# Two projections of a layer as one 2x2 block product with seven products, and the work around it in another order

## The chip, the cores and the metric

The kernel runs on one core of a Trainium2 chip. The metric is the device time of one execution in microseconds. The kernel before takes 1845.83 us, the median of three runs (1845.75 to 1846.41). TensorE (PE) multiplies, VectorE (DVE) and ScalarE (ACT) work elementwise, GpSimd (POOL) does small work and issues some DMAs, SyncE (SP) issues the other DMAs. Each engine works through its own queue in a fixed order.

## The reference

One sequence of 512 tokens, width 1024, float32, goes through a first block (an mLSTM beside a stick-breaking attention, then an MLP of width 4096) and then through two hybrid layers. The change is in the hybrid layers:

```python
h = rms_norm_2(x, g_pre)
proj = jnp.einsum('bsd,de->bse', h, w_in)
q_h, f_h, i_h, z_h, q_a, k_a, v_a, z_a = jnp.split(proj, SPLIT_POINTS, axis=-1)
o_h = hgrn2(q_h, f_h, i_h, lb)           # 8 recurrent heads of 128
o_h = rms_norm_2(o_h, g_head).reshape(B, S, HG_WIDTH) * jax.nn.silu(z_h)
...                                      # rotary on q_a, k_a
o_a = sliding_window_attention(q_a, k_a, v_a, sinks) * jax.nn.silu(z_a)
y = jnp.einsum('bse,ed->bsd', jnp.concatenate([o_h, o_a], axis=-1), w_out)
return x + rms_norm_2(y, g_post)
```

The parts q, f, i and z of the recurrent heads are 1024 columns each: i holds the values, z the output gate.

## The kernel before, in words

Every float32 operand of a large product is split into two halves of reduced precision, hi and lo, and a product is three matmuls (hi by hi, hi by lo, lo by hi) that add up in one PSUM bank (`mm3`, lines 143 to 151). A projection of 512 columns (`gemm_a` gives columns by tokens, `gemm_b` tokens by columns) has four tiles of 128x512, each of 8 parts of the depth: 4 x 8 x 3 = 96 matmuls of 512 columns. The tiles (`mm`) rotate through two PSUM banks, so the third waits until the first has been evacuated.

Weights come in pieces of 512 KB (`wr`, six buffers) by SyncE. ScalarE casts each to its high half (`wh`, line 137) and VectorE subtracts for the low half (`wl`, five buffers, line 138).

In `seven` a product of a 2x2 block matrix of x by a 2x2 block matrix of weights is done with seven block products of 24 matmuls instead of eight, as Strassen's method does, with sums of blocks of x and of the weights. The weight sums are made by DMA: a piece is loaded by SyncE (`piece`, line 181), and GpSimd issues a DMA that adds a second piece onto it in place (`plus`, line 185). The MLP's `down2` uses it three times.

A layer begins while the step before it ends: for each block of 128 tokens, as soon as its last sum is there, `prep` squares it, GpSimd makes the norm's factor (lines 293 and 115), VectorE scales (283), TensorE transposes (286), ScalarE casts the high half `hh` (258) and VectorE makes the low half `hl` (259). In layer 1 the block's sum first gets the layer's norm (716) and the old x, which is read back from memory (715). Then come i(0) (`proj_i`, values, four heads), which goes by token blocks, q(0) and f(0), and then zh(0), i(1), q(1), f(1) with the first four recurrent heads (`hgrn`) beside them at higher priority; key and value, zh(1), q and gate of the attention with the other four heads; the rest with the attention pairs (`swa_pair`); the output product.

The order in each engine's queue is set when the program is built: a scheduler takes priorities (those of evacuations, weight splits and heads are raised) and its own estimate of times. On the chip each queue then runs in that order, whatever is ready.

## Time and profile before

| | |
|---|---|
| time, median of three runs | 1845.83 us |
| the profiled execution | 1846.15 us, span 1844.2 us |
| TensorE busy | 1809.8 us, 98% |
| VectorE, ScalarE, GpSimd busy | 58%, 46%, 9% |
| layer 0, layer 1 | 861 to 1348 us, 1348 to 1844 us |
| DMA, whole span | 195.80 MB, 106 GB/s |

The spans of the layers are read from the first matmul of i(0) and the last of the output product. Matmul records overlap their successors, so the cost of one is the time between two starts, or a stretch without gaps divided by its count.

### The profile page before, as it was taken

How to read it: one execution, taken by the hardware profiler on the slowest of the kernel's cores; microseconds unless marked ns; L12 is line 12 of the kernel's file. 1: busy time of each engine (PE TensorE's matmuls, PEld its weight loads, DVE VectorE, ACT ScalarE, POOL GpSimd, SP SyncE). 2: the span in 40 equal slices, each digit the busy share in tenths (PEclk: the TensorE clock that was granted, in tenths of full speed). 3: DMA queues.
4: the chain of work that ended last, by engine and by line, in shares of the span. 5: the costliest groups of instructions: out<-in, count | busy, mean ns of one | idle time of the engine just before them, and what ended most of it. 6: DMA issues, size and time to landing. Idle time of an engine off the chain costs nothing.

```text
span 1844.2 us, 29460 instructions
## 1 busy us (share of the span) xinstructions
PE 1809.8 (98%) x11624; PEld 1484.8 (81%) x11624; DVE 1069.2 (58%) x2179; ACT 849.8 (46%) x1696; POOL 161.6 (9%) x215
## 2 busy tenths in 40 slices
PE   7999999999999999999999999999999999999998
PEld 5777788787798888878888888888878888888886
DVE  4364445546555575575474766755365648575733
ACT  4546644343443344443343436655343345375741
POOL 1001111020001110110000001100120000101002
PEclk9999999999999999999999999999999999999999
DMA  7342432221425855474331232322352223322222
GB/s 216 70 103 70 97 92 69 69 92 46 149 91 128 204 146 167 122 187 146 94 116 52 87 131 88 103 86 75 110 164 92 88 75 98 127 87 75 75 69 91
DMA packets 111602, 195.80 MB, mean 106 GB/s; under 512 B 9441, under 2 KB 20065, under 8 KB 111465
## 3 DMA queue, kind: packets, MB, share of 16 engines
q1 hardware_dynamic: 104936, 181.35, 31.9%
q0 software_dynamic: 6528, 12.58, 4.0%
q8 instruction: 91, 1.49, 0.3%
q14 instruction: 47, 0.38, 0.1%
HBM read 179.21 MB, written 14.70 MB: 105 GB/s over the span
## 4 chain that ended last, share of the span: by engine, by line
PE 53%; ACT 1%; DVE 1%; issue 0%; POOL 0%; DMA 0%; DVEq 0%; POOLq 0%; SPq 0%; ACTq 0%
PE mm L151 14%; PE mm L150 14%; PE mm L149 13%; PE xc L634 2%; PE xa L602 1%; PE xc L636 1%; PE xb L624 1%; PE xc L498 1%; PE xa L443 1%; PE xb L470 1%; PE xc L490 1%; PE xc L500 1%; PE xb L626 1%; PE xa L432 0%; PE mt L536 0%
## 5 line engine op out<-in xcount | busy, mean ns | idle before, releaser
L138 DVE TENSOR_TENSOR wl<-wr,wh 128x1024 fp32r<-128x1024 f32 (+1 forms) x248 | 298.3, 1211 | 119.6 <-PE mm L150 72.2
L149 PE MATMUL mm<-wh,hh 128*128 128x512 f32 (+1 forms) x896 | 348.2, 389 | 5.8 <-ACT hh L258 3.0
L150 PE MATMUL mm<-wl,hh 128*128 128x512 f32 (+1 forms) x896 | 348.3, 389 | 0.8 <-DVE wl L138 0.8
L151 PE MATMUL mm<-wh,hl 128*128 128x512 f32 (+1 forms) x896 | 346.9, 390 | 0.0
L137 ACT CAST wh<-wr 128x1024 fp32r<-128x1024 f32 (+1 forms) x248 | 255.0, 1038 | 143.8 <-PE mm L151 72.2
L149 PE MATMUL mm<-hh,wh 128*128 128x512 f32 x640 | 254.8, 398 | 1.3 <-ACT pg L801 1.3
L151 PE MATMUL mm<-hh,wl 128*128 128x512 f32 x640 | 253.5, 396 | 1.8 <-DVE wl L138 1.7
L150 PE MATMUL mm<-hl,wh 128*128 128x512 f32 x640 | 253.1, 395 | 0.0
L149 PEld LDWEIGHTS mm<-wh,hh 128*128 128x128 f32 x896 | 169.1, 189 | 40.1 <-ACT hh L258 3.5
L150 PEld LDWEIGHTS mm<-wl,hh 128*128 128x128 f32 x896 | 168.9, 189 | 33.5 <-DVE wl L138 1.7
L151 PEld LDWEIGHTS mm<-wh,hl 128*128 128x128 f32 x896 | 167.8, 189 | 31.4 <-DVE hl L259 0.5
L151 PEld LDWEIGHTS mm<-hh,wl 128*128 128x128 f32 x640 | 120.8, 189 | 28.8 <-DVE wl L138 3.0
L149 PEld LDWEIGHTS mm<-hh,wh 128*128 128x128 f32 x640 | 120.8, 189 | 27.4 <-ACT pg L801 2.6
L150 PEld LDWEIGHTS mm<-hl,wh 128*128 128x128 f32 x640 | 121.0, 189 | 24.9 <-issue 0.2
L149 PE MATMUL mm<-qd,wh 128*128 128x512 f32 (+1 forms) x288 | 105.5, 366 | 0.0
L150 PE MATMUL mm<-qd,wh 128*128 128x512 f32 (+1 forms) x288 | 105.4, 366 | 0.0
L151 PE MATMUL mm<-qd,wl 128*128 128x512 f32 (+1 forms) x288 | 104.9, 365 | 0.0
L115 POOL TENSOR_TENSOR sm<-sm,nhalf 128x4 f32<-128x4 f32 (+1 forms) x64 | 60.2, 941 | 504.6 <-DVE sm L507 327.9
L149 PE MATMUL mm<-wh,qd 128*128 128x512 f32 x192 | 75.2, 392 | 1.2 <-DVE qd L1198 0.8
L151 PE MATMUL mm<-wh,qd 128*128 128x512 f32 x192 | 74.7, 389 | 0.0
L150 PE MATMUL mm<-wl,qd 128*128 128x512 f32 x192 | 74.7, 389 | 0.0
L610 ACT ACTIVATE pg<-pg,sm 128x256 f32<-128x256 f32 (+1 forms) x128 | 60.9, 478 | 15.5 <-DVE sm L608 15.4
(312 smaller groups left out, 2927.8 us busy)
## 6 DMA issues: line engine op xcount, KB each, us to landing
wr<-in_w_in_dram SPq DMA_DIRECT2D x160, 512.0 KB, 4.7
wr<-in_w_out_dram SPq DMA_DIRECT2D x40, 512.0 KB, 4.0
wr<-in_w_down_dram SPq DMA_DIRECT2D x38, 512.0 KB, 5.4
wr<-in_w_up_dram SPq DMA_DIRECT2D x32, 512.0 KB, 5.1
wr<-in_w_down_dram POOLq DMA_DIRECT2D x24, 512.0 KB, 7.8
zh<-pg SPq DMA_DIRECT2D x16, 256.0 KB, 2.0
pg<-zh SPq DMA_DIRECT2D x16, 256.0 KB, 2.8
za<-pg SPq DMA_DIRECT2D x16, 256.0 KB, 2.0
```

Source lines behind the costliest of these rows:

```text
L115: self.nc.gpsimd.tensor_tensor(y, ms, e, ALU.pow)
L137: nc.scalar.copy(hi, raw)
L138: nc.vector.tensor_tensor(lo, raw, hi.bitcast(F32), ALU.subtract)
L149: nc.tensor.matmul(ps, sh, mh, start=(k == 0), stop=False)
L150: nc.tensor.matmul(ps, sh, ml, start=False, stop=False)
L151: nc.tensor.matmul(ps, sl, mh, start=False, stop=(k == n - 1))
L443: nc.tensor.matmul(pl[32 * j:32 * j + 32, o0 + 32 * c:o0 + 32 * c + 32], k[:, o:o + 32], q[:, o:o + 32])
L470: nc.tensor.matmul(pb[0:64, 64 * c:64 * c + 64], k[:, o:o + 64], q[:, o + 64:o + 128])
L490: nc.tensor.matmul(pS[:, c, :], kt[:, c, :], v[c][:, vc])
L498: nc.tensor.matmul(po[:, c, :], ST[:, c, :], v[c][:, vc], start=True, stop=(c == 0))
L610: nc.scalar.activation(prw, prw, AF.Exp, bias=pn[:, n:n + 1], scale=-1.0, accum_out=den[:, n:n + 1])
L634: nc.tensor.matmul(o, va[0][:, n, vv], pT[n // 2][:, n % 2, 0:P], start=True, stop=(n == 0))
```

## The change

In each layer i(c) and zh(c) become one block product, `pair(c)`: x is cut into 2x2 blocks (256 tokens by 512 of depth), the weights into the 512 columns of i and of zh. `pair` has 7 x 24 = 168 matmuls. It needs sums of blocks of x, which `sides` makes once for both pairs of a layer: four whole sums of hi and lo, four sums and differences, four splits, all 128x1024; the results stay in a pool of their own whose space the recurrent heads use later. q(0) comes first in a layer, in two halves of 256 tokens; then `sides`, f(0), pair(0) and pair(1); then q(1) and f(1) with the first heads. The order of weights in the plan of `seven` changes in one place, also for the MLP.

```diff
@@ seven @@
-                ("00", "1", c, True, (0, 0, ALU.add)), ("10", "2", x, True, (0, 0, ALU.add)),
-                ("Y", "6", c, False, (0, 1, ALU.subtract)), ("V", "7", c, False, (1, 1, ALU.subtract)),
+                ("00", "1", c, True, (0, 0, ALU.add)), ("Y", "6", c, False, (0, 1, ALU.subtract)),
+                ("10", "2", x, True, (0, 0, ALU.add)), ("V", "7", c, False, (1, 1, ALU.subtract)),
...
+    def sides(self, T, pool, tmp):
...
+        a11, a12, a21, a22 = raw
+        whole(a21, part(0, 1))
+        whole(a22, part(1, 1))
+        nc.vector.tensor_tensor(a22, a21, a22, ALU.subtract)
+        keep("5", a22)
+        whole(a11, part(0, 0))
+        whole(a12, part(1, 0))
+        nc.vector.tensor_tensor(a22, a22, a11, ALU.subtract)
+        nc.vector.tensor_tensor(a12, a22, a12, ALU.add)
+        keep("3", a12)
+        keep("6", a22)
+        nc.vector.tensor_tensor(a21, a11, a21, ALU.subtract)
+        keep("7", a21)
+        return ops
...
@@ layer, proj_q @@
-            K.gemm_a(win[:, c * S:(c + 1) * S], evac)
+            K.gemm_a(win[:, c * S:(c + 1) * S], evac, 2 if c == 0 else 1)
...
@@ layer, pair in place of proj_i and proj_zh @@
+        def pair(c, ops):
...
+            def acc(i, t, j, ps, op):
+                tb = 2 * i + t
+                if j:
+                    v = quad[:, tb, :]
+                    if tb in seen:
+                        nc.vector.tensor_tensor(v, v, ps, op)
+                    else:
+                        seen.add(tb)
+                        nc.scalar.copy(v, ps)
+                    return
+                z = ps
+                if tb in zc:
+                    z = zc[tb]
+                    nc.vector.tensor_tensor(z, z, ps, op)
...
+            K.seven(blk, ops.get, acc)
...
@@ layer, order @@
-        proj_i(0)
         proj_q(0)
-        proj_f(0)
+        with tc.tile_pool(name="sd", bufs=1, reuse_waits="tile") as sd:
+            ops = K.sides(K.T, sd, [K.quad(), K.quad()])
+            proj_f(0)
+            pair(0, ops)
+            pair(1, ops)
+        K.lp2 = lctx.enter_context(tc.tile_pool(name="lp2", bufs=1, reuse_waits="tile"))
...
         p0 = mark()
-        proj_zh(0)
-        proj_i(1)
         proj_q(1)
         proj_f(1)
...
         proj_kv()
-        proj_zh(1)
         proj_qa(0)
         proj_za(0)
```

How the queues move is shown at three places. VectorE at the start of layer 0, before; the three rows with `mm` as a source are evacuations of q(0)'s tiles, those of line 138 weight splits:

```order
709 L138 TENSOR_TENSOR wl_6878<-wr_6875,wh_6877 128x1024
710 L138 TENSOR_TENSOR wl_6884<-wr_6881,wh_6883 128x1024
711 L138 TENSOR_TENSOR wl_6890<-wr_6887,wh_6889 128x1024
712 L138 TENSOR_TENSOR wl_7009<-wr_7006,wh_7008 128x1024
713 L378 SCALAR_TENSOR_TENSOR qd_6868<-mm_6893,om_6720,pg_6918 128x512
714 L378 SCALAR_TENSOR_TENSOR qd_6868<-mm_6921,om_6720,pg_6946 128x512
715 L378 SCALAR_TENSOR_TENSOR qd_6868<-mm_6949,om_6720,pg_6974 128x512
716 L138 TENSOR_TENSOR wl_7015<-wr_7012,wh_7014 128x1024
717 L138 TENSOR_TENSOR wl_7021<-wr_7018,wh_7020 128x1024
```

VectorE at the same place after the change; line 292 is the low half (259 before), 412 the evacuation of a half tile of q(0) (378 before), 258 a whole sum of x, 346 and 347 the casts of a mask:

```order
688 L292 TENSOR_TENSOR hl_6305<-xb_6639,hh_6303 128x4x128
689 L292 TENSOR_TENSOR hl_6306<-xa_6647,hh_6304 128x4x128
692 L292 TENSOR_TENSOR hl_6305<-xb_6680,hh_6303 128x4x128
693 L292 TENSOR_TENSOR hl_6306<-xa_6688,hh_6304 128x4x128
694 L412 SCALAR_TENSOR_TENSOR qd_6731<-mm_6756,om_6720,pg_6781 128x256
695 L258 TENSOR_TENSOR qd_6984<-hh_6303,hl_6305 128x4x256
696 L258 TENSOR_TENSOR qd_6983<-hh_6303,hl_6305 128x4x256
697 L258 TENSOR_TENSOR qd_6983<-hh_6304,hl_6306 128x4x256
698 L258 TENSOR_TENSOR qd_6984<-hh_6304,hl_6306 128x4x256
699 L346 CAST hgmask<-ST_6701 128x512
700 L347 CAST hgmask<-ST_6703 128x128
701 L412 SCALAR_TENSOR_TENSOR qd_6731<-mm_6784,om_6720,pg_6809 128x256
```

The evacuations of q(0)'s first two tiles now stand behind the low half of block 3, with the four whole sums between them.

VectorE at the start of layer 1, before: the last block's norm and addition of x (716), its scaling (283) and the last low halves (259):

```order
1376 L716 SCALAR_TENSOR_TENSOR pg_10974<-pg_10974,sm_11668,pg_11670 128x512
1377 L716 SCALAR_TENSOR_TENSOR pg_10975<-pg_10975,sm_11668,pg_11674 128x512
1378 L283 SCALAR_TENSOR_TENSOR pg_11678<-pg_10974,sm_11686,pg_11260 128x512
1379 L283 SCALAR_TENSOR_TENSOR pg_11679<-pg_10975,sm_11686,pg_11262 128x512
1380 L259 TENSOR_TENSOR hl_11258<-xb_11621,hh_11256 128x4x128
1381 L259 TENSOR_TENSOR hl_11259<-xa_11629,hh_11257 128x4x128
1382 L259 TENSOR_TENSOR hl_11258<-xb_11689,hh_11256 128x4x128
1383 L259 TENSOR_TENSOR hl_11259<-xa_11697,hh_11257 128x4x128
```

The same place after the change (768 is the norm and the addition of x, 716 before; 316 the scaling):

```order
1420 L768 SCALAR_TENSOR_TENSOR pg_11155<-pg_11155,sm_11849,pg_11851 128x512
1421 L768 SCALAR_TENSOR_TENSOR pg_11156<-pg_11156,sm_11849,pg_11855 128x512
1422 L292 TENSOR_TENSOR hl_11439<-xb_11802,hh_11437 128x4x128
1423 L292 TENSOR_TENSOR hl_11440<-xa_11810,hh_11438 128x4x128
1424 L412 SCALAR_TENSOR_TENSOR qd_11913<-mm_11938,om_11889,pg_11963 128x256
1425 L316 SCALAR_TENSOR_TENSOR pg_11859<-pg_11155,sm_11867,pg_11441 128x512
1426 L316 SCALAR_TENSOR_TENSOR pg_11860<-pg_11156,sm_11867,pg_11443 128x512
1427 L412 SCALAR_TENSOR_TENSOR qd_11913<-mm_11966,om_11889,pg_11991 128x256
1428 L412 SCALAR_TENSOR_TENSOR qd_11913<-mm_11994,om_11889,pg_12019 128x256
1429 L292 TENSOR_TENSOR hl_11439<-xb_11870,hh_11437 128x4x128
1430 L292 TENSOR_TENSOR hl_11440<-xa_11878,hh_11438 128x4x128
1431 L258 TENSOR_TENSOR qd_12166<-hh_11437,hl_11439 128x4x256
```

The evacuations of the first three tiles of q(0) now stand behind the additions of the last block's x.

GpSimd at the same time, before; lines 293 and 115 are the norms' factors, 708 the last step of the layer's output:

```order
177 L115 TENSOR_TENSOR sm_11600<-sm_11598,nhalf 128x1
178 L293 TENSOR_SCALAR sm_11616<-sm_11612,sm_11613 128x1
179 L115 TENSOR_TENSOR sm_11618<-sm_11616,nhalf 128x1
180 L708 TENSOR_TENSOR pg_10975<-pg_10975,pg_11254 128x512
181 L293 TENSOR_SCALAR sm_11666<-sm_11404,sm_11662 128x1
182 L115 TENSOR_TENSOR sm_11668<-sm_11666,nhalf 128x1
183 L293 TENSOR_SCALAR sm_11684<-sm_11680,sm_11681 128x1
184 L115 TENSOR_TENSOR sm_11686<-sm_11684,nhalf 128x1
185 L115 TENSOR_TENSOR sm_12865<-sm_12863,nhalf 128x4
```

After the change, with 326 for 293, 760 for 708, and 185 for an accumulating DMA:

```order
193 L115 TENSOR_TENSOR sm_11781<-sm_11779,nhalf 128x1
194 L185 DMA wr_12329<-in_w_in_dram 128x2x512
195 L326 TENSOR_SCALAR sm_11797<-sm_11793,sm_11794 128x1
196 L115 TENSOR_TENSOR sm_11799<-sm_11797,nhalf 128x1
197 L760 TENSOR_TENSOR pg_11156<-pg_11156,pg_11435 128x512
198 L326 TENSOR_SCALAR sm_11847<-sm_11585,sm_11843 128x1
199 L185 DMA wr_12336<-in_w_in_dram 128x2x512
200 L115 TENSOR_TENSOR sm_11849<-sm_11847,nhalf 128x1
201 L326 TENSOR_SCALAR sm_11865<-sm_11861,sm_11862 128x1
202 L115 TENSOR_TENSOR sm_11867<-sm_11865,nhalf 128x1
203 L185 DMA wr_12329<-in_w_in_dram 128x2x512
```

Two accumulating DMAs of pair(0) now stand among the factors of the last two blocks.

## Rows read from the trace of the kernel before

**Rows 1.** The page, part 1: busy time, share of the span, instructions.
```profile
span 1844.2 us, 29460 instructions
...
PE 1809.8 (98%) x11624; PEld 1484.8 (81%) x11624; DVE 1069.2 (58%) x2179; ACT 849.8 (46%) x1696; POOL 161.6 (9%) x215
```

**Rows 2.** Busy us by stretch; counts of instructions begun; clock, DMA share, GB/s.
```profile
core 0: us, PE busy (x) PEld busy (x) DVE busy (x) ACT busy (x) POOL busy (x), PEclk, DMA share, GB/s
861.45:886.00 24.55, 24.55 (x121) 20.46 (x120) 15.66 (x34) 11.57 (x18) 2.35 (x6) 1.00 0.34 103
1347.60:1376.10 28.50, 24.78 (x122) 20.34 (x121) 18.31 (x23) 12.31 (x23) 4.84 (x7) 1.00 0.41 130
535.00:547.00 12.00, 12.00 (x103) 12.00 (x102) 3.32 (x6) 3.35 (x6) 0.00 (x0) 1.00 0.00 1
600.00:700.00 100.00, 99.98 (x441) 82.45 (x441) 68.04 (x71) 43.33 (x47) 14.48 (x12) 1.00 0.72 177
1225.00:1285.00 60.00, 58.26 (x364) 47.90 (x365) 41.44 (x137) 41.43 (x113) 0.00 (x0) 1.00 0.24 81
```

**Rows 3.** One of three like groups of TensorE from 535 to 547 us: shape, count.
```profile
L150 PE MATMUL mm<-qd,wh 128*128 128x256 f32 x35 | 9.9, 283 | 0.0
```

**Rows 4.** Timeline at layer 0's start: start us, us, engine, line, what.
```profile
861.45 0.39 PE L149 MATMUL mm<-wh,hh 128*128 128x512 f32 x1
...
861.91 0.60 PE L286 MATMUL xb<-ident,wk 128*128 128x128 f32 x4
...
862.70 0.47 PE L151 MATMUL mm<-wh,hl 128*128 128x512 f32 x1
...
866.29 0.68 DVE L259 TENSOR_TENSOR hl<-xa,hh 128x512 fp32r<-128x512 f32 x1
...
873.63 0.69 DVE L259 TENSOR_TENSOR hl<-xa,hh 128x512 fp32r<-128x512 f32 x1 [0.18 <-ACT hh L258]
...
886.00 0.39 PE L149 MATMUL mm<-hh,wh 128*128 128x512 f32 x1
```

**Rows 5.** Timeline and waits (total us, times, longest) at layer 1's start.
```profile
1353.84 0.81 SPq L715 DMA_DIRECT2D pg<-xs  x2
...
1354.20 0.67 DVE L259 TENSOR_TENSOR hl<-xa,hh 128x512 fp32r<-128x512 f32 x1
...
1360.11 1.41 DVE L716 SCALAR_TENSOR_TENSOR pg<-pg,sm,pg 128x512 f32<-128x512 f32 x2 [3.09 <-DMA pg<-xs]
...
PE xb L286 <- DVE pg L283: 3.7, 1, 3.7
```

**Rows 6.** Groups of instructions (mean ns after the comma), and one table load.
```profile
L138 DVE TENSOR_TENSOR wl<-wr,wh 128x1024 fp32r<-128x1024 f32 (+1 forms) x248 | 298.3, 1211 | 119.6 <-PE mm L150 72.2
...
L478 DVE TENSOR_TENSOR qd<-qd,T 128x256 f32<-128x256 f32 x48 | 20.2, 421 | 6.3 <-PE xb L461 5.0 <-PE xb L470 1.2
...
L407 DVE TENSOR_TENSOR pg<-mm,pg 128x512 f32<-128x512 f32 x8 | 5.5, 690 | 9.5 <-ACT pg L406 9.5
...
875.93 1.28 ACT L349 ACT_TABLE_LOAD   x1
```

**Rows 7.** Three stretches of the MLP's products; then line 185's accumulating DMAs.
```profile
595.00:605.00 10.00, 10.00 (x46) 8.29 (x45) 7.30 (x8) 4.39 (x5) 2.40 (x2) 1.00 0.83 263
605.00:615.00 10.00, 10.00 (x45) 8.27 (x45) 5.54 (x7) 4.67 (x5) 2.42 (x2) 1.00 1.09 205
685.00:695.00 10.00, 10.00 (x46) 8.28 (x45) 6.97 (x8) 4.68 (x5) 3.08 (x3) 1.00 1.08 214
...
L185 POOL DMA_DIRECT2D wr<-in_w_down_dram x24: 1194/1203/1466, 553.9 to 795.2; - x24
...
DMA to landing us min/median/max: 5.9/7.8/10.7
```

**Rows 8.** The heads' stretch, and one of its parts.
```profile
917.00:1285.00 368.00, 366.15 (x3320) 303.11 (x3320) 238.94 (x656) 190.40 (x461) 23.30 (x20) 1.00 0.28 91
1030.00:1090.00 60.00, 59.90 (x977) 49.95 (x976) 44.63 (x135) 27.49 (x73) 4.34 (x6) 1.00 0.25 81
```

More of the change, by code (lines that the diff above doesn't have):

```diff
@@ L194, in split_w, with seven @@
         return [(hi[:, k, :], lo[:, k, :]) for k in range(2)]
-    def seven(self, blk, aop, acc):
+    def seven(self, blk, aop, acc, wx=None):
         nc = self.nc
@@ L245, in seven, with part, whole, keep @@
                     acc(i, t, j, bank[t], op)
+    def sides(self, T, pool, tmp):
+        nc = self.nc
+        def part(i, t):
+            return [a[i][:, :, 256 * t:256 * t + 256] for a in T]
+        ops = {"1": part(0, 0), "2": part(1, 0), "4": part(1, 1)}
+        raw = [q[:, :, 256 * e:256 * e + 256] for q in tmp for e in range(2)]
+        def whole(o, p):
+            nc.vector.tensor_tensor(o, p[0].bitcast(F32), p[1].bitcast(F32), ALU.add)
+        def keep(name, src):
+            o = pool.tile([P, 2, 4, 256], F32R, name=self.nm("sd"), tag="sd" + name)
+            self.split(o[:, 0], o[:, 1], src)
+            ops[name] = (o[:, 0], o[:, 1])
+        a11, a12, a21, a22 = raw
[12 more added lines that the diff above has]
+        return ops
     def new_T(self):
@@ L322, in layer @@
     if True:
+        lctx = ExitStack()
         def page(tag, bufs):
-            return K.lp.tile([P, S], F32, name=K.nm("pg"), tag=tag, bufs=bufs)
+            return (K.lp if tag in ("ev", "f", "zs", "va") else K.lp2).tile([P, S], F32, name=K.nm("pg"), tag=tag, bufs=bufs)
         def ev():
@@ L371, in proj_q, with evac @@
             quad = K.quad()
[L373 removed]
+            def evac(m, ps, t=slice(0, S)):
                 h = 4 * c + m
[L375 removed]
+                sg = ev()[:, :t.stop - t.start]
                 nc.scalar.activation(sg, ps, AF.Sigmoid)
[L377 to L380 removed]
+                nc.vector.scalar_tensor_tensor(quad[:, m, t], ps, om[:, h:h + 1], sg, ALU.mult, ALU.mult)
+                qh[h] = quad[:, m, :]
+            K.gemm_a(win[:, c * S:(c + 1) * S], evac, 2 if c == 0 else 1)
         def proj_f(c):
@@ L419, in hgrn @@
             nc.sync.dma_start(out=zs, in_=zh_d[:, h * P:(h + 1) * P].rearrange("(c p) d -> p c d", p=P))
-            qx = K.lp.tile([P, 16, 48], F32, name=K.nm("qx"), tag="qx", bufs=1)
+            qx = K.lp2.tile([P, 16, 48], F32, name=K.nm("qx"), tag="qx", bufs=1)
             nc.scalar.copy(qx[:, :, 0:32], q.rearrange("p (n t) -> p n t", n=16))
@@ L579, in proj_za @@
             K.gemm_a(win[:, 5 * D + 256 + c * S:5 * D + 256 + (c + 1) * S], evac)
-        oa = [page("f", 4) for _ in range(4)] + [page("on", 8) for _ in range(4)]
         def swa_pair(p):
@@ L640, in layer @@
         mark = lambda: tc.cur_priority
-        proj_i(0)
         proj_q(0)
-        proj_f(0)
+        with tc.tile_pool(name="sd", bufs=1, reuse_waits="tile") as sd:
[4 more added lines that the diff above has]
+        K.lp2 = lctx.enter_context(tc.tile_pool(name="lp2", bufs=1, reuse_waits="tile"))
+        oa = [page("f", 4) for _ in range(4)] + [page("on", 8) for _ in range(4)]
         p0 = mark()
-        proj_zh(0)
-        proj_i(1)
         proj_q(1)
@@ L723, in layer @@
         if gnext is not None:
-            K.hT = K.pairs(TN)
+            K.hT, K.T = K.pairs(TN), TN
+        lctx.close()
 def block1(K, xd, prm, win, wout, wup, wdown, bif, gmix, gmlp, out, gnext):
@@ L1218, in block1 @@
         down(7, x7)
-        K.hT = K.pairs(TN)
+        K.hT, K.T = K.pairs(TN), TN
 _INS = ["x", "cst", "prm", "w_in", "w_out", "w_up", "w_down", "b_if", "norm_mix_g", "norm_mlp_g",
```

28 lines of the change are left out of this document (12 added, 16 removed).

## The prediction

> **What bounds the kernel now.** I read the busy times first [rows 1]. TensorE is busy 1809.8 of 1844.2 us, VectorE 58%, ScalarE 46%: the reader is to see that only TensorE can be the bound, and that the 34 us in which it is idle are all that other engines can give back. Then I read stretches [rows 2]. From 600 to 700 us it ran 441 matmuls of 512 columns in 99.98 us without a gap, at a granted clock of 1.00, so one costs 0.227 us; a removed matmul is worth that much, and an added wait costs its full length. In the layers the same table shows where waits lie. The value projection that opens layer 0 (861.45 to 886.0) has none. The one that opens layer 1 (1347.6 to 1376.1) has 3.7 us, and the waits of that stretch name it: a transpose for the norm's scaled x [rows 5]. The attention pairs (1225 to 1285) lose 1.7 us. So the change takes matmuls from stretches that are full; what matters is whether the stretches that it builds stay full.
>
> **What is removed.** A pair by seven block products has 168 matmuls where two projections have 192. Two pairs in each of two layers: 96 matmuls x 0.227 = -21.8 us. This term is sure, since nothing in [rows 2] lets TensorE run faster than its stream.
>
> **The query projection in token halves.** q(0) issues 192 matmuls of 256 columns for 96 of 512. The kernel has such halves once, in the MLP: 103 of them began in 12.00 us [rows 2, 3], 0.117 us each. 192 x 0.117 - 96 x 0.227 = 22.4 - 21.8 = +0.6 us a layer.
>
> **The start of layer 0.** This is the first disputed term. Before, the layer opened with i(0), which goes by token block: its first tile needs block 0 of the transposed x alone, and blocks 1 to 3 are made beside it. Now q(0) opens it, and each tile of its first half needs blocks 0 and 1, hi and lo. TensorE came free at 861.45, and block 1's last low half began at 866.29 in VectorE's queue [rows 4]; the work ahead of it (two weight splits, the adds into x, the scaling of block 2) is still ahead of it in the new order. I take 866.5 as the true start of q(0); transposes fill part of the 5 us, the rest is idle. From there a tile is 24 x 0.117 = 2.8 us, and the last block's eight transposes are 0.9 (eight took 0.79, from 861.91 to 862.70 [rows 4]). There are two banks for such tiles, so tile n+2 waits for the evacuation of tile n. In VectorE's new order four whole adds of 128x1024 stand between the evacuations of m0 and m1, and two sums, one add and two low halves between those of m2 and m3. An operation of that size is 1.21 us [rows 6]. Block 3's low half began at 873.63 before [rows 4]; in the new order only block 2's stands between it and block 1's: 867.1 + 1.4 (scaling of block 3, two operations of 128x512 like those in [rows 5]) + 1.2 (block 2's halves) + 1.5 (its transposes and a cast) + 1.2 = 872.4. The evacuation of m0 follows to 872.8, four adds and two small casts to 878.1, that of m1 to 878.5 (0.42 each [rows 6]). m0 and m1 share 866.5 to 873.0, m2 ends at 875.8, m3 waits 2.7 us. m3 and m4 end at 884.1; five operations after m2's evacuation take VectorE to 885.2, so m5 waits 1.1. The rest keeps up: q(0) ends at 893.6 where i(0) ended at 886.0, +7.6 us, the 0.6 of the halves in it. Lower bound: the halves of block 1 two us earlier and no wait for a bank, 864.5 + 0.9 + 22.4 = 887.8, +1.8. Upper: GpSimd issues two accumulating DMAs ahead of the norm's row sums, at 1.2 us each [rows 7], +10.0.
>
> The Trainium skill ("Perfetto Trace Analysis", section Matmuls) says that independent groups of matmuls should rotate through PSUM banks so that the evacuation of one overlaps the matmuls of the next. By it alone the 3.8 us of bank waits would be nothing and the layer would start 3.8 us earlier. The kernel does rotate, through two banks, and no row of before shows whole adds between two evacuations, so no run here shows yet which holds; the sum above goes by the order of VectorE's queue.
>
> **The start of layer 1.** Here x of block 3 comes back from memory: its load was issued at 1353.84, and the add that waits for it began at 1360.11 [rows 5]. Before, that cost 3.7 us, since i(0) had done three blocks by then. Now TensorE, free at 1347.6 [rows 2] and with 0.9 of transposes at hand, waits from 1348.5 to 1354.2 for block 1 (its low half of xa began at 1354.20 before [rows 5]). m0 and m1 last until 1360.7. The evacuation of m0 stands in VectorE's order behind the add that waits for the load, the two low halves of block 2, and on ScalarE behind a table load of 1.28 us [rows 6]: 1360.1 + 1.4 + 1.3 + 1.3 + 0.6 + 0.4 = 1365.1, so m2 starts 4.4 us late. Then 6 tiles x 2.8, 0.9 of transposes and again about 1.9 behind adds: 1384.7. i(0) ended at 1376.1: +8.6, and 0.4 for one of the two accumulating DMAs that GpSimd issues between two of its row sums, +9.0. Lower bound: only the wait for block 1, 1354.2 + 0.9 + 22.4 = 1377.5, +1.4. Upper: both DMA issues on the chain, +11.4.
>
> **The pairs' weights.** A pair moves 18 pieces of 512 KB where its two projections moved 8, eight of the 18 as accumulating DMAs. Two pairs are 36 x 0.524 = 18.9 MB in 336 x 0.227 = 76.3 us, 247 GB/s. By the order eight of the 36 can be in before the pair starts, since six buffers are free while q(0) runs; the other 28 ask for 193 GB/s. The block products of the MLP moved 263 GB/s in their best 10 us, and 205 and 214 in the two in which the engines were full [rows 7], without a stall of TensorE. So the stream is just enough; I take +1 us a layer, between 0 and +5 (two pieces ahead instead of eight: 17.8 MB at 205 GB/s are 87 us, 10.6 more than the matmuls, of which I let what arrives during f(0) cover half).
>
> **Recurrent and attention heads with less cover.** Three projections (zh twice, i once) leave the stretch in which heads run; it had 366.15 us of TensorE and 238.94 of VectorE in 368 [rows 8], 65%. Three times 21.8 less, and 20 less for VectorE (12 weight splits at 1.21, eight evacuations of zh at 0.69 [rows 6]), make 301 and 219: 73%. From 1030 to 1090 VectorE was at 74% and TensorE lost 0.1 [rows 8], so I take +1 a layer. From 1225 to 1285 both other engines were at 69% and it lost 1.74 us in 60; at that rate 301 us lose 8.7. Bounds 0 and +8.7 a layer. The sums of x themselves (12 operations of VectorE, 14.5 us) and the pairs' evacuations lie beside q(0), f(0) and the pairs; in the layer's first projection VectorE was at 64% [rows 2].
>
> In the MLP two weight sums change places: no matmul changes and no stall was there; nothing, within 1 us.
>
> **Sum.** -21.8 + 7.6 + 9.0 + 2 x 1 + 2 x 1 = -1.2 us. The profiled run took 1846.15 us, 1844.2 of them span; the median of the runs shown is 1845.83, 0.3 lower. 1846.15 - 1.2 = 1845: the gain of the seven products is eaten at the layers' starts.
>
> **Rivals.** First, the starts cost little. The waits that I add up are serial in my reading, and small shifts of VectorE's work can dissolve them. At the lower bounds they are 3.2 us for both layers instead of 16.6, and the sum is -14.6 with the 4 us of the other terms, -18.6 without: 1827 to 1832. In the middle, starts of 8 us, 1836. For it: before, TensorE lost just 3.7 us at two starts. Against it: q(0) does need two blocks, and the order of the queues is fixed. I give it 0.34.
>
> Second, slower: cover. If the heads lose TensorE time at the rate of the attention pairs, the term is 2 x 8.7 = 17.4 instead of 2: 1845 - 2 + 17 = 1860. It decides from VectorE at about three quarters with ScalarE alike. For it: the attention pairs do lose time at that share, since a chain there passes through three engines in turn. Against: 1030 to 1090. I give it 0.16.
>
> Third, the weights. The Trainium skill ("DMA: Bandwidth & Descriptors", section Issuing engines are not separate DMA queues) says that DMAs started by different engines run on the same 16 DMA engines and interleave. The trace agrees: with GpSimd's and SyncE's pieces together the DMA share was 1.09 at 205 GB/s, less moved than at a share of 0.83 [rows 7]. Accumulates then compete with the pieces that they follow, each takes 7.8 us to land (10.7 at most), and a chain of piece, first and second sum stands before two of the seven weights. At the upper bound, 5 us a layer, the time is 1845 - 2 + 10 = 1853. I give it 0.12; the forecast keeps 0.38.
>
> **How the numbers follow.** Between faster and slower I count 0.2%, 3.7 us, which is about what a measurement of this kernel can tell from no change. The forecast, 1845 with 1840 to 1850 as its own range, gives 0.23 to no change, 0.09 to faster and 0.06 to slower. The first rival is faster; the other two slower, but for 0.02 of the weights' case. Faster 0.43, same 0.25, slower 0.32. The range leaves out one in ten at each side: 1830, in the first rival, to 1859, in the second.
>
> **What would show it.** Right: in each layer the first matmul group of q(0) idles 3 to 5 us for a low half, a group of q(0) waits for an evacuation behind whole adds, and q(0) ends 7 to 10 us later after the layer's start than i(0) did. The pairs run 168 matmuls in 38 us each, gaps under 1 us. Wrong: q(0) without gaps (the time falls to 1830), gaps before the sixth and seventh product for an accumulating DMA, or idle TensorE in the heads' stretch.

## The result, and the profile after

The changed kernel takes 1891.06 us (median of four runs, 1888.7 to 1900.05) where the kernel before took 1846.12 in the same sitting: a ratio of 1.0248, with a 95% interval of 1.0228 to 1.0267. The forecast was 1845, the range 1830 to 1859. The profiled run took 1891.77 us, 45.6 more than the one before. The runs of one kernel differ in the clock: the slowest of these four had a mean granted clock of 0.980, the fastest 0.987.

The page of the changed kernel, part 1:

```profile
span 1889.9 us, 29941 instructions
...
PE 1814.6 (96%) x11720; PEld 1493.5 (79%) x11720; DVE 1142.3 (60%) x2259; ACT 894.9 (47%) x1752; POOL 204.8 (11%) x247
```

TensorE is busy 1814.6 us, 4.8 more than in [rows 1], though 96 matmuls of 512 columns are gone, and it is idle 75 us instead of 34. Both grew. The mean granted clock tells most of why busy time grew (span, clock of the core):

```profile
core: us from the first to the last instruction, mean granted TensorE clock
core 0: 1889.9 us, clock 0.987
```

It was 0.997 before. In 1889.9 us that is a deficit of 24.6 us against 5.5 then: up to 19 us more, where busy time without the removed 21.8 us grew by 26.6.

To see where the time went I took the ends of the last evacuation of each stage in both traces, and took from the stages of before what the change moved into the pairs (a projection is 96 x 0.2275 = 21.8 us; 282.3 is 347.8 less three of them):

| stretch | before | after | difference | forecast |
|---|---|---|---|---|
| start to the MLP's third last sum | 857.1 | 861.1 | +4.0 | 0 |
| from there to the end of f(0), layer 0 | 77.1 - 21.8 | 69.3 | +14.0 | +7.6 |
| two pairs (four projections before) | 87.4 | 87.4 | 0.0 | -10.9 + 1 |
| from there to the last attention pair | 282.3 | 288.3 | +6.0 | +1 |
| to the end of f(0), layer 1 | 142.2 - 21.8 | 131.3 | +10.9 | +9.0 |
| two pairs | 87.4 | 91.9 | +4.5 | -10.9 + 1 |
| to the last attention pair | 282.0 | 288.2 | +6.2 | +1 |

The sum is 45.6. No stage gained. The marks are ends of evacuations, so some work falls into a neighbouring stretch: 15 matmuls of q(1), 3.4 us, run between those of the pairs in each layer, and 160 small matmuls of the heads that ran ahead of the end of f(0) before now stand behind it.

TensorE's busy time and clock in five of these stretches of the changed kernel (layer 0's start, pairs and heads, layer 1's start and pairs; the clock is the third number from the end):

```profile
core 0: us, PE busy (x) PEld busy (x) DVE busy (x) ACT busy (x) POOL busy (x), PEclk, DMA share, GB/s
861.10:930.40 69.30, 60.66 (x350) 54.19 (x349) 45.89 (x76) 31.56 (x51) 11.74 (x16) 0.93 0.37 91
930.40:1017.80 87.40, 82.33 (x354) 66.07 (x353) 47.63 (x50) 40.40 (x50) 14.65 (x12) 1.00 0.91 240
1017.80:1306.10 288.30, 281.43 (x2938) 234.04 (x2937) 212.68 (x627) 167.85 (x430) 25.35 (x20) 0.99 0.25 80
1306.10:1437.40 131.30, 119.69 (x615) 102.55 (x614) 70.61 (x85) 50.81 (x86) 25.27 (x28) 0.97 0.40 116
1437.40:1529.40 92.00, 86.36 (x355) 69.28 (x354) 47.78 (x51) 40.38 (x50) 14.70 (x12) 0.94 0.88 229
```

TensorE was idle 8.6, 5.1, 6.9, 11.6 and 5.6 us in them. Before, it was idle 0 in layer 0's start, 1.9 in its heads' stretch and 3.7 in layer 1's start, at a clock of 1.00 in all three. The pairs of the two layers have nearly the same idle time; the 4.5 us more in layer 1 are the clock.

**The starts.** TensorE at layer 0's start, changed kernel (start, length; in brackets the idle time before and what ended it):

```profile
867.92 0.66 PE L319 MATMUL xa<-ident,wk 128*128 128x128 f32 x4
872.27 0.64 PE L149 MATMUL mm<-hh,wh 128*128 128x256 f32 x2 [3.70 <-DVE wk L316]
...
888.11 0.39 PE L149 MATMUL mm<-hh,wh 128*128 128x256 f32 x1 [1.60 <-DVE qd L412]
...
896.27 0.51 PE L149 MATMUL mm<-hh,wh 128*128 128x256 f32 x1 [2.14 <-DVE qd L412]
```

To compare with the start of [rows 4], where no wait stood: q(0) waits 3.7 us at its first matmuls (the profile names the scaling of a block, 316, as what ended it), and later 1.6 and 2.1 for evacuations (412), as the prediction had it. It came on top that the blocks themselves were late. GpSimd in the same trace:

```profile
862.29 1.21 POOL L185 DMA_DIRECT2D wr<-in_w_in_dram  x1 [63.85 <-DMA xs<-qd]
863.59 0.29 POOL L326 TENSOR_SCALAR sm<-sm,sm 128x1 f32<-128x1 f32 x1
```

GpSimd had stood for 63.9 us, at the end for an accumulating DMA of pair(0), whose piece SyncE had issued only at 856.0, behind the weights of f(0) and the stores of x (the profile names a store of x, not the piece, as what ended the wait; e2 below tests it). The norm factor of block 0 stood behind it and was begun at 863.59, 9.5 us after the same instruction before; 4 of these come from the MLP. And after such waits the clock was low. Five short stretches of the changed kernel, in the same columns:

```profile
870.00:875.00 5.00, 2.08 (x9) 1.78 (x10) 4.84 (x8) 3.61 (x10) 2.52 (x3) 0.75 0.76 224
875.00:880.00 5.00, 5.00 (x28) 5.00 (x27) 2.94 (x7) 0.89 (x2) 0.97 (x3) 0.57 0.77 146
880.00:885.00 5.00, 5.00 (x44) 5.00 (x43) 4.03 (x6) 1.84 (x4) 0.35 (x2) 1.00 0.46 135
1390.00:1395.00 5.00, 3.45 (x17) 3.45 (x18) 2.20 (x5) 1.24 (x3) 0.00 (x0) 0.66 0.04 16
1505.00:1510.00 5.00, 4.95 (x12) 3.90 (x13) 1.92 (x2) 1.57 (x2) 0.00 (x0) 0.50 0.78 247
```

The first holds the end of the 3.7 us above, the last two those of waits of 5.4 us (until 1391.55) and 3.6 us (until 1505.05). From 875 to 880 TensorE is busy without a gap and begins 28 instructions, in the next 5 us 44: a clock of 0.57 lies between the two levels, 1.2 and 2.4 GHz, and 1.00 is the upper.

**The pairs.** Waits (total us, times, longest) from 930 to 1018 us, the pairs of layer 0:

```profile
POOL wr L185 <- DMA wr<-in_w_in_dram: 22.2, 2, 11.3
ACT wh L192 <- DMA wr<-in_w_in_dram: 20.2, 5, 7.4
...
DVE wl L193 <- ACT wh L192: 6.7, 4, 4.5
```

ScalarE stood for 20 us at weights in transfer. Evacuations of products sit behind such casts in its queue, so a late piece held up TensorE twice: as a weight and through a bank. ScalarE's timeline:

```profile
952.29 1.05 ACT L192 CAST wh<-wr 128x1024 fp32r<-128x1024 f32 x1 [7.38 <-DMA wr<-in_w_in_dram]
953.25 0.57 ACT L445 COPY qd<-mm 128x512 f32<-128x512 f32 x1
...
965.39 1.04 ACT L192 CAST wh<-wr 128x1024 fp32r<-128x1024 f32 x1 [5.62 <-DMA wr<-in_w_in_dram]
```

The last of these casts waited 5.6 us, and TensorE behind it 2.6. Line 185's accumulating DMAs of the pairs, and the time to landing of all that line issued:

```profile
L185 POOL DMA_DIRECT2D wr<-in_w_in_dram x32: 1194/1242/2706, 862.3 to 1492.4; - x32
...
DMA to landing us min/median/max: 5.5/7.8/15.1
```

To [rows 7] answer these stretches of the pairs (DMA share and GB/s at the end):

```profile
935.00:975.00 40.00, 37.04 (x159) 29.44 (x158) 21.15 (x23) 17.42 (x22) 9.71 (x8) 1.00 0.95 225
975.00:1010.00 35.00, 32.89 (x143) 26.42 (x142) 21.76 (x24) 18.46 (x24) 4.94 (x4) 1.00 0.98 277
```

The engines were full (0.95 and 0.98) at 225 and 277 GB/s, and TensorE idle 5 us of 75. Two waits make up most of it: the 2.6 above for a cast of a weight, and 2.1 for a copy of a product that stood behind such casts on ScalarE.

**The heads.** Two stretches of 20 us after f(1), layer 0:

```profile
1078.00:1098.00 20.00, 20.00 (x401) 17.57 (x400) 18.83 (x55) 10.36 (x28) 2.69 (x3) 1.00 0.22 65
1098.00:1118.00 20.00, 16.85 (x214) 13.28 (x213) 13.79 (x49) 5.04 (x20) 3.52 (x3) 0.91 0.21 70
```

In the first VectorE is busy 94% and TensorE never waits. In the second TensorE is idle 3 us and its clock 0.91. Its timeline shows the reason:

```profile
1103.75 0.39 PE L149 MATMUL mm<-wh,hh 128*128 128x512 f32 x1
...
1109.19 0.68 PE L522 MATMUL xb<-qd,qd 128*64 128x64 f32 x8 [1.03 <-ACT ST L517]
...
1116.29 0.50 PE L149 MATMUL mm<-wh,hh 128*128 128x512 f32 x1 [0.87 <-DVE pg L575]
```

Two projection tiles run until 1104 with one short break, while the heads' small matmuls stand behind them and VectorE is idle for 4.9 us; then only the heads' chain is left, and the next tile waits for its bank until 1116.29.

**The MLP.** With Y one product earlier:

```profile
619.52 0.47 PE L227 MATMUL xa<-wh,ao 128*128 128x512 f32 x1 [3.18 <-ACT wh L192]
```

A second wait, of 1.9 us, ends at 704.87. Before, no product waited at either place.

### The profile page after: what moved, and what is told of

Read it like the earlier page. It is cut to its first block, busy times and chain, and to the rows that moved or that the text cites. A ratio compares the mean times of both kernels' runs of the same rounds, so it can differ in the third digit from the quotient of the medians.

```text
span 1889.9 us, 29941 instructions
## 1 busy us (share of the span) xinstructions
PE 1814.6 (96%) x11720; PEld 1493.5 (79%) x11720; DVE 1142.3 (60%) x2259; ACT 894.9 (47%) x1752; POOL 204.8 (11%) x247
## 5 line engine op out<-in xcount | busy, mean ns | idle before, releaser
L149 PE MATMUL mm<-hh,wh 128*128 128x512 f32 (+1 forms) x704 | 269.2, 383 | 20.5 <-DVE qd L412 10.6
L151 PE MATMUL mm<-hh,wl 128*128 128x512 f32 (+1 forms) x704 | 265.7, 378 | 1.7 <-DVE wl L138 1.6
L150 PE MATMUL mm<-hl,wh 128*128 128x512 f32 (+1 forms) x704 | 266.5, 379 | 0.0
L149 PE MATMUL mm<-wh,hh 128*128 128x512 f32 (+1 forms) x640 | 249.8, 391 | 5.2 <-ACT hh L291 3.2
L150 PE MATMUL mm<-wl,hh 128*128 128x512 f32 (+1 forms) x640 | 247.4, 387 | 1.2 <-DVE wl L138 1.2
L151 PE MATMUL mm<-wh,hl 128*128 128x512 f32 (+1 forms) x640 | 245.6, 388 | 0.0
L192 ACT CAST wh<-wr 128x1024 fp32r<-128x1024 f32 x98 | 102.1, 1052 | 116.4 <-DMA wr<-in_w_in_dram 42.6
L193 DVE TENSOR_TENSOR wl<-wr,wh 128x1024 fp32r<-128x1024 f32 x98 | 119.4, 1223 | 57.0 <-PE xa L228 33.8
L149 PEld LDWEIGHTS mm<-wh,hh 128*128 128x128 f32 x640 | 121.2, 189 | 30.4 <-ACT hh L291 3.8
L149 PE MATMUL mm<-wh,qd 128*128 128x512 f32 x192 | 74.7, 390 | 0.3 <-DVE qd L1251 0.3
```

Of the source, the lines that this page charges most:

```text
L149: nc.tensor.matmul(ps, sh, mh, start=(k == 0), stop=False)
L150: nc.tensor.matmul(ps, sh, ml, start=False, stop=False)
L151: nc.tensor.matmul(ps, sl, mh, start=False, stop=(k == n - 1))
L192: nc.scalar.copy(hi, raw)
L193: nc.vector.tensor_tensor(lo, raw, hi.bitcast(F32), ALU.subtract)
```

## The experiments

Each time is a median, with that of the kernel before in the same sitting. Stretches are those of the table.

**Old plan everywhere.** The two lines of the plan as before.

> The changed kernel with the old order of weights in the plan of the seven products (10 before Y), in the MLP and in the pairs. Theory A: the new order makes the MLP's products wait for the accumulating DMA of Y, which now has two products instead of three to land in; it cost the 5 us by which the MLP ended later (last add into x begun at 870.6 instead of 864.0, the one before the last block's at 852.2 instead of 847.1), and something in the pairs, which ran 86.8 and 91.8 us for 76.3 us of matmuls. Then the time falls by 5 to 15 us, to 1876 to 1886, and no matmul near 616 or 703 us waits for a weight half. Rival: the later end of the MLP comes from transfers that the next layer's first pieces add at its end; then the waits at 616 and 703 stay and the time stays within 3 us of 1891.

Measured: 1893.83 (before 1847.66). The MLP's third last sum ended at 854.1, 7.0 earlier, with no wait at 616 or 703; but the pairs took 95.0 and 95.9 instead of 87.4 and 91.9. Theory A holds for the waits in the MLP and fails for the time. In the pairs the old order brings nothing either. Their stretch holds more of the work that follows (43 matmuls of q(1) instead of 26, and 32 of the heads), and the heads' stretch got 1.4 and 2.5 us shorter; pairs and heads together took 381.9 and 381.6 us instead of 375.7 and 380.1. The mean clock was 0.984 instead of 0.987, 5.7 us more of deficit.

**Old plan in the MLP only.**

```diff
...
+        plan = new if first_y else new[:3] + [new[4], new[3]] + new[5:]
...
```

> The changed kernel with the old order of weights in the MLP's three products and the new order in the pairs. From e1, where the MLP ended 6.9 us earlier and the pairs took 7.6 and 4.0 us more: here the MLP ends at 864 to 865 as in the kernel before, the pairs keep 87 and 92 us, and the time is 1891 - 6 = 1885. Rival: what e1 gave back in the pairs came from starting earlier (same transfers, less time for them) and not from the plan; then the pairs get longer here too, and the time stays at 1889 to 1893.

Measured: 1889.60 (1847.25). The MLP ended at 854.8 (-6.3), the pairs took 88.4 and 93.4, the heads 290.8 and 290.6. So the MLP's waits are the plan's. Against e1, which differs in the pairs' order alone, pairs and heads together took 763.3 us in the two layers for 763.5: that order shows no effect. But the time fell by 1.5, not 6: in the profiled run (1894.2) the starts lost 1.4 us, the pairs 2.5 and the heads 4.9. TensorE was idle 73.9 us in it, 1.4 less than in the changed kernel; the clock was 0.982, a deficit of 34.1 us instead of 24.6. What the MLP gained was lost as clock; why the clock was lower is not shown.

**Norm factors first.**

```diff
+        if after is not None:
+            self.nc.gpsimd.tensor_scalar(t[:, 0, 0:1], after, 0.0, None, ALU.add)
...
-            pair(0, ops)
+            pair(0, ops, K.last)
```

> The changed kernel in which the two first pieces of pair(0) wait until the norm factor of the layer's last token block is there (GpSimd writes one column of each piece's buffer from that factor; the piece then overwrites it). So no accumulating DMA of pair(0) stands in GpSimd's queue ahead of a norm factor. Theory: at layer 0 the factor of block 0 came at 863.6 instead of 854.1 because GpSimd stood at an accumulating DMA until 862.3, whose piece stood in SyncE's queue behind stores of x; without it q(0) starts in earnest about 8.5 us earlier in layer 0 and 2 to 4 in layer 1, where the two DMA issues stand among the factors of the last two blocks, and the clock falls less: 1891 - 11 to 16 = 1875 to 1880. Rival: q(0) waits for block 1 anyway (the five us that the prediction had) and for its evacuations behind the sums of x; then only 4 to 6 us are gained, 1885 to 1887. If the pairs' pieces then come too late, the pairs get longer than 87 and 92 us and eat the gain.

Measured: 1890.85 (1847.66). The starts took 65.1 and 125.4, 4.2 and 5.9 less: 10 us, near the 10.5 to 12.5 expected there, but divided otherwise (8.5 in layer 0, 2 to 4 in layer 1). TensorE in layer 0:

```profile
867.06 0.39 PE L149 MATMUL mm<-hh,wh 128*128 128x256 f32 x1 [0.79 <-ACT hh L293]
...
870.18 0.39 PE L150 MATMUL mm<-hl,wh 128*128 128x256 f32 x1 [1.34 <-DVE hl L294]
...
878.14 0.38 PE L149 MATMUL mm<-hh,wh 128*128 128x256 f32 x1 [1.32 <-DVE qd L415]
...
888.71 0.39 PE L149 MATMUL mm<-hh,wh 128*128 128x256 f32 x1 [3.64 <-DVE qd L415]
```

The wait for block 1 is now 0.8 and 1.3 us; the waits for evacuations stay, 1.3 and 3.6. But the pairs took 91.5 and 91.1 and the heads 291.9 and 292.2, 10.9 us more together. The time did not move. Layer 0's start and its heads:

```profile
860.90:926.00 65.10, 57.27 (x346) 50.77 (x345) 44.54 (x74) 31.29 (x51) 9.85 (x16) 0.97 0.41 102
1017.50:1309.40 291.90, 285.37 (x2938) 236.01 (x2937) 211.96 (x627) 164.84 (x428) 23.73 (x20) 0.98 0.25 80
```

In the start TensorE was idle 7.8 us, only 0.8 less than in the changed kernel; the rest of the 4.2 is the clock, 0.97 instead of 0.93. (In layer 1's start the idle time fell by 5.6.) In the heads it was idle 6.5 us instead of 6.9: the waits together did not grow there, and most of the loss is the clock, 0.98 instead of 0.99 of 290 us.

**No sums of x.** Four operands are blocks of x.

```diff
+        for n, p in (("5", (0, 1)), ("3", (0, 0)), ("6", (1, 0)), ("7", (1, 1))):
+            ops[n] = part(*p)
+        return ops
```

> The changed kernel without the sums of x: the operands of four of the seven products are blocks of x themselves, so the result is another one, while every matmul, weight sum and evacuation of a product stays. VectorE loses 12 operations of 128x1024 in each layer (14.5 us), ScalarE four casts. Theory: q(0)'s tiles waited 1.6 and 2.1 us in layer 0 and about 3 in layer 1 for evacuations that stood behind those operations, and the clock fell once after it; without them 5 to 9 us in all are gained, 1882 to 1886. Rival: the waits of q(0) come from the late low halves alone and move to the next thing; then less than 3 us.

Measured: 1886.87 (1847.66), runs from 1882.4 to 1894.8. The starts took 62.9 and 129.3, 6.4 and 2.0 less: 8.4, in the range of the theory. The time fell by 4, within the spread of the runs.

**Norm factors first and no sums of x, with the old plan in the MLP.**

> The changed kernel with the old plan in the MLP, the first pieces of pair(0) after the last norm factor, and without the sums of x (four operands are blocks of x themselves, so the result is another one). What is left at the starts is what my prediction had as the wait of q(0) for block 1. The starts (from the third last add of the MLP to the end of f(0), and from the last attention pair to it in layer 1) took 69.3 and 131.3 us in the changed kernel, 55.3 and 120.4 in the kernel before less one projection. Theory: GpSimd's queue (4.2 and 5.9 in e2) and the sums (6.4 and 2.0 in e3) add up, and 3 to 4 us are left in each layer: 58.7 and 123.4. Rival: they overlap, each hiding part of the other; then 62 and 126 or more are left, since q(0)'s need of two blocks is the larger part. The time itself: 1891 - 5 - 18 + up to 8 for pairs and heads, which got longer in e2: 1868 to 1876.

Measured: 1876.51 (1847.86). The starts took 65.0 and 123.0. In layer 1 the two parts add up and 2.6 us are left. In layer 0 they do not, and 9.7 us are left: a new wait of 4.9 us, until 884.0, ate part of the gain. VectorE there:

```profile
882.83 0.17 DVE L406 TENSOR_SCALAR nsnk<-snk 128x16 f32<-128x16 f32 x1 [3.68 <-DMA snk<-in_sinks_dram]
...
883.44 0.48 DVE L419 SCALAR_TENSOR_TENSOR qd<-mm,om,pg 128x256 f32<-128x256 f32 x1
```

The evacuation of a half tile stood behind an operation on the attention sinks, which waited 3.7 us for a small load of the layer's set-up. Any instruction in VectorE's queue that waits for a transfer holds the evacuations behind it, not the sums alone.

**No weight sums in the pairs.** The accumulating DMAs of the pairs are left out.

> The changed kernel without the accumulating DMAs of the pairs (the MLP keeps its own): the weight sums are left out, so the result is another one; 20 pieces per layer instead of 36, all matmuls, splits and evacuations as they were. Theory D: the pairs wait for weights. They took 87.4 and 92.0 us from the last tile of f(0) to their own last tile, for 76.3 us of matmuls, and ScalarE stood at casts of pieces still in transfer, with evacuations queued behind them. Without the sums they take 76 to 78 us, 25 us less in both layers, and since GpSimd no longer stands at a DMA ahead of the norm factors, the starts gain the 10 us that e2 showed there: 1891 - 35 = 1856. Rival: the pairs are held by their evacuations (40 sums on VectorE and copies on ScalarE for two rotating banks); then they stay above 83 us and the time above 1870.

Measured: 1875.07 (1847.25). The pairs took 81.5 us in both layers, 5.9 and 10.4 less, and TensorE has no gap in them:

```profile
925.00:965.00 40.00, 40.00 (x175) 32.47 (x174) 21.73 (x23) 18.71 (x23) 0.00 (x0) 1.00 0.48 148
965.00:1005.00 40.00, 40.00 (x175) 32.61 (x174) 25.43 (x27) 21.84 (x28) 0.00 (x0) 1.00 0.60 192
```

So the pairs waited for weights, or for evacuations that stood behind them. The run takes away 16 of 36 transfers and the dependence of one on another at once, so it does not tell which of the two held them. Less came back than the 25 us expected, since without any wait a pair's matmul still costs 0.231 us from start to start (77.7 us for 336), not 0.227, and the 3.4 us of q(1)'s matmuls were never lost. The starts gained 12.9. The heads took 292.1 and 293.8: without those transfers they are not shorter, so late transfers are not what holds them.

**Less cover.** The kernel before with zh(0), i(1), zh(1) in a row after f(0).

> The kernel before with only the place of three projections changed: zh(0), i(1) and zh(1) run right after f(0), ahead of the recurrent heads, as ordinary projections with all their matmuls. q(1), f(1) and the attention's projections are what is left beside the heads. Theory B: the heads and attention pairs need those matmuls as cover, so the stretch from q(1) to the last attention pair gets 6 us longer in each layer, as in the changed kernel (289 us against 283), and the time is 1846 + 12 = 1858. Rival: with the attention pairs' rate of loss (1.7 in 60 us) it would be 1863; if the 6 us in the changed kernel came from transfers or its later buffers, the time stays within 3 us of 1846.

Measured: 1850.46 (1847.66), a ratio of 1.0012 (0.9999 to 1.0024). The profiled run took 1854.0, 5 of it in the MLP, which is the same code; the stretch from f(0) to the last attention pair took 349.5 and 348.8 instead of 347.8 and 347.5. Theory B falls in this form: the heads still began at 925 us, beside zh(0), because their priority is higher.

**Heads late as well.** Their space is held until zh(1) has been evacuated.

```diff
...
+                for t in hold:
+                    nc.vector.tensor_scalar(t[:, 0, 0, tb:tb + 1], sg[:, 0:1], 0.0, None, ALU.add)
...
```

> The kernel of e4 (the kernel before with zh(0), i(1) and zh(1) ahead of q(1)) in which, besides, the heads' pages lie in space that zh(1)'s evacuation still writes to (a pool of 32 KB whose four tiles get a column each), as the sums of x do in the changed kernel. Eight tiny VectorE operations a layer more and no other work. In e4 the heads still began at 925 us beside zh(0), and the stretch from f(0) to the last attention pair took 349.5 us for 347.8: cover as such cost nearly nothing, against my theory. Theory C: in the changed kernel the heads cannot begin before pair(1) has read the sums (first head instruction on TensorE at 1018.4, after the pairs), so the same heads have 92 us less in which to lie beside matmuls. Then the stretch gets 5 to 7 us longer than in e4, in both layers, and the time is 1850 + 12 = 1862. Rival: what is longer there comes from the pairs' late transfers (key and value weights, zh read back); then it stays at 1850.

Measured: 1850.03 (1847.25). The first head matmul came at 1005 us, as meant, and the stretch took 351.0 and 350.9: +1.5 and +2.1 over e4, +3.2 and +3.4 over before, half of the 6 us in the changed kernel. But the small head matmuls that moved behind the end of f(0) made the starts shorter, 74.5 and 140.5 us instead of 77.1 and 142.2: start and stretch together took 0.5 and 1.7 us more than before. Theory C falls too. The same two places as in the changed kernel:

```profile
1078.00:1098.00 20.00, 20.00 (x283) 15.96 (x282) 17.36 (x50) 6.13 (x22) 3.88 (x3) 1.00 0.38 120
1098.00:1118.00 20.00, 20.00 (x244) 16.45 (x243) 18.34 (x43) 9.59 (x24) 5.70 (x4) 1.00 0.40 117
```

Here TensorE runs 283 and 244 matmuls without a gap, and VectorE is at 87 and 92%.

**q(1) ahead of the pairs**, with the old MLP plan, norm factors first and the sums after f(0).

> The changed kernel with four edits together: the old plan in the MLP (worth 6 us), the first pieces of pair(0) after the last norm factor (10 at the starts in e2), the sums of x issued after f(0) instead of after q(0), and q(1) ahead of the pairs, so that the sums and first transfers lie beside f(0) and q(1) (e3 had 8 for the sums). If these add up: 1891 - 24 = 1867, less up to 5 for the pairs, whose first transfers now have 44 us, and more up to 8 for heads that have lost q(1) as cover: 1862 to 1875. If the pairs' stream and the late heads are all that is left beyond the kernel before, the starts (from the MLP's end to the end of f(0), one projection fewer than before) are within 3 to 5 us of 48 us. Rival: the starts keep 8 us or more since q(0) needs two blocks; then above 1875.

Measured: 1886.15 (1847.25). The starts took 62.0 and 128.2; the pairs with q(1) 106.3 in both layers (84.5 without its 21.8), the rest up to the last attention pair 278.7 and 271.8, which is 300.5 and 293.6 with q(1), up to 12 more than in the changed kernel. What the pairs and the starts gained, the heads without q(1) lost. The gains did not add up.

**One pair, with the old opening.**

```diff
...
+        proj_i(0)
         proj_q(0)
...
-            pair(0, ops)
+            proj_zh(0)
             pair(1, ops)
```

> The changed kernel with one pair a layer instead of two, and with the opening of the kernel before: i(0), q(0) whole and f(0) as ordinary projections, the sums of x issued after f(0), zh(0) ordinary, pair(1), then the heads; the old plan in the MLP. Theory: without q(0) at the front and with the sums beside zh(0) the layers' starts are those of the kernel before (69.6 us from the MLP's end to the end of f(0), 142.2 from the last attention pair to layer 1's), and one pair whose first pieces arrive during zh(0) no longer waits for weights. What is left is 24 matmuls fewer in each layer (5.5 us) against heads that begin late (1 to 6 us a layer): 1847 - 11 + 2 to 12 = 1838 to 1848. Rival: the pair's transfers are late even alone, or the sums hold up zh(0)'s evacuations; then the stretch from f(0) to the end of the pair is over 62 us (21.8 + 38.2 = 60 without waits) and the time is over 1850.

Measured: 1862.41 (1847.86), 1.0078 (1.0060 to 1.0095). The starts are those of before (69.7 to the end of f(0) from the MLP's last sum, 143.5 in layer 1), and the pair waits 2.7 us for weights. But the stretch from f(0) to the last attention pair took 356.5 and 352.9, where 342.3 was due. Up to the end of the pair it took 66.3 and 65.7 us, over the 62 that the rival named, and the time is over its 1850: a pair's transfers are late even alone, though the waits are less than half of the excess. After the pair it took 290.2 and 287.2, 7.9 and 5.2 more than in the kernel before. Three stretches of it:

```profile
1056.00:1076.00 20.00, 20.00 (x369) 18.09 (x368) 18.52 (x64) 10.61 (x29) 3.21 (x4) 1.00 0.22 64
1076.00:1096.00 20.00, 17.40 (x265) 13.42 (x263) 13.71 (x43) 4.42 (x19) 2.23 (x2) 0.97 0.31 101
1096.00:1116.00 20.00, 18.68 (x188) 14.95 (x189) 13.68 (x36) 7.89 (x23) 6.48 (x4) 0.86 0.15 43
```

The hole of the changed kernel is here too, in the second. So neither the front of the layer nor the second pair is needed for the loss in the heads.

**The price of an idle stretch.** The kernel before, with a chain of VectorE operations ahead of one evacuation in each layer.

```diff
+                for _ in range(16 if h == 2 else 0):
+                    nc.vector.tensor_scalar(sg, sg, 1.0, 0.0, ALU.mult, ALU.add)
```

> The kernel before with 16 more VectorE operations of 128x512 (multiply by one) in a chain ahead of the evacuation of q(0)'s third tile in each layer, about 9 us, so that TensorE has to wait for that bank some 4 us. It measures the price of an idle stretch of TensorE by itself. Theory: an idle stretch of 3 to 5 us is followed by several us at half the granted clock, as after the starts of the changed kernel (0.5 from 874 to 878 us, after 3.7 us of idleness), so each costs about 3 us more than its own length: 1847 + 2 x (4 + 3) = 1861. Rival: the low clock belongs to the mix of short gaps and half-width matmuls there; then the clock stays at 1.00, as it did after the 3.7 us at 1364 in the kernel before, and the time is 1847 + 8 = 1855.

Measured: 1857.33 (1847.86), +9.5. In the profiled run (1860.57) layer 0's start got 4.6 us longer, layer 1's 7.2. The wait in layer 0 was

```profile
912.62 0.71 PE L149 MATMUL mm<-hh,wh 128*128 128x512 f32 x1 [2.72 <-DVE qd L380]
```

and the clock around it (three stretches of 5 us):

```profile
910.00:915.00 5.00, 2.38 (x6) 1.90 (x7) 4.83 (x11) 1.30 (x2) 0.00 (x0) 0.77 0.93 315
915.00:920.00 5.00, 5.00 (x21) 4.03 (x20) 2.66 (x6) 0.00 (x0) 0.00 (x0) 0.89 0.06 20
920.00:925.00 5.00, 5.00 (x23) 4.13 (x23) 3.03 (x10) 1.51 (x3) 0.00 (x0) 1.00 0.00 0
```

2.7 us of idleness, then 1.15 + 0.55 us of clock not granted: 4.4 of the 4.6 us by which that start got longer. The wait in layer 1 was 2.7 us as well, with a clock of 0.66 in the 5 us around it, another 1.7. The rest of the 7.2 comes from an old wait, that for the norm's scaled x [rows 5]. It was 3.4 us here, until 1370.86, and the clock after it was low:

```profile
1370.00:1375.00 5.00, 4.14 (x14) 3.58 (x15) 3.96 (x6) 1.50 (x3) 0.00 (x0) 0.51 0.01 3
1375.00:1380.00 5.00, 5.00 (x19) 3.99 (x19) 0.00 (x0) 0.00 (x0) 0.00 (x0) 0.81 0.00 0
```

That is 3.4 us of clock, so this run's +9.5 is not the price of the two new waits alone. The rival that the clock stays is out for this run, but the price is no rule: after the same old wait, 3.7 us at 1364 in the kernel before, the clock stayed at 1.00, and after 3.1 us in e7 it was 0.69 for 5 us.

## Why the prediction was wrong

The likeliest case said that the starts eat the gain. They ate more than that, two further terms, priced at 1 us a layer each, cost more again, and the clock, which no term had, is up to 19 of the 46 us by which the time missed the forecast.

- **What is removed, -21.8 us.** Right to 3 us: 336 matmuls of a layer's pairs cost 0.231 us each in e5.
- **"... an added wait costs its full length."** This premise, ahead of all terms, failed. The deficit of clock rose from 5.5 to 24.6 us, most of it in the stretches after waits.
- **The starts, 16.6 us forecast, 24.9 measured.** The mechanism is the one named, low halves and evacuations behind sums, and e2 and e3 show both. The waits even had the size: TensorE was idle 16.5 us more in the two starts, and its waits for evacuations were 3.7 and 6.8 us, where I had 3.8 and 6.3. The other 8 us are the clock (0.93 and 0.97). That the sum of the waits fits is partly luck: I let GpSimd's accumulating DMA cost its issue, 1.2 us, as the upper bound (which for layer 1 should have been 11.0, not 11.4), and it cost the wait for its piece, which stood in SyncE's queue behind stores of x. Without it block 0's factor came at 857.9 (e2), with it at 863.6, and TensorE was idle 0.8 and 5.6 us less.
- **The pairs' weights, +1 a layer forecast.** This is the term that failed most. TensorE was idle 5.1 and 5.6 us in the pairs, about my upper bound, and the clock after these waits took some 5 us more in layer 1. e5 gives 5.9 and 10.4 us to the weight sums. I compared a mean demand (247, or 193 GB/s) with a mean supply (205 to 263) and took the stream to be just enough. The engines were indeed full, and that alone may be the reason. But there is also a chain that a mean doesn't hold: three sums of a pair are made in place, one after the other, in two buffers (I counted two); each waits until the cast and the subtraction have read the sum before, then lands 7.8 us later (15.1 at most, where [rows 7] had 10.7), and then the cast queues on ScalarE. How much each of the two, full engines and chain, cost is open: no run separates them. The MLP's products that I took as evidence stand one at a time, with ordinary matmuls between one product and the next; two pairs follow each other. The Trainium skill's rule that DMAs of all issuing engines share the 16 DMA engines ("DMA: Bandwidth & Descriptors", section Issuing engines are not separate DMA queues) spoke for this rival, and the trace agrees: the pairs ran at a DMA share of 0.95 and 0.98. I gave the rival 0.12.
- **Heads with less cover, +1 a layer forecast, 6 measured.** The rival had 8.7 and the reason "cover". e4 and e7 show that the same cover costs 0.5 to 2 us in another arrangement, e5 and e9 that time is lost with no sums of weights or with one pair. Most of the loss has a place, a block of two projection tiles that starves the heads' chain, and the price of the low clock on it: 3 us idle and 1.8 of clock from 1098 to 1118. Why the scheduler puts the queue this way in the kernels with a pair, and not in e7, is open; a kernel that changes only that order wasn't tried.
- **The MLP's plan, 0 within 1 us; +4 measured** (7.0 and 6.3 came back in e1 and e6). Y's sum has two products to land in where it had three: a transfer that I took to have time enough, as in the pairs. The waits are shown, near 619 and 704 us in all four profiles with the new plan there and in none of the nine others; the size is not sure. The third last sum ended at 857.4 to 863.8 us with the new plan, at 854.1 to 856.3 in the five changed kernels with the old one, and at 857.1 to 862.4 in the four profiles of the kernel before and its variants.

The rivals on the slower side gave 1853 and 1860, each alone. What happened is all of them and the forecast's own case together: the chances were split over cases as if they excluded each other. Two of the prediction's signs of being wrong came, gaps in the pairs and idle TensorE in the heads, beside its signs of being right.
